# Layer 0's memory keys and values in one pass, x loaded early into the residual's tile, zeros multiplied ahead, and wide products ahead of narrow ones in every weight-stationary group

## The chip, the cores and the metric

The kernel runs on one core of one Trainium2 chip. The metric is the device time of one execution in microseconds (us), as the median of several executions. A difference of under about 0.2% cannot be told from no change by such a measurement.

## The reference, cut to what matters

Two layers. Each projects x (256 rows of 2048) by an input matrix, runs three groups of heads and maps their concatenation back. The change touches the memory group's keys and values, which depend on `mem` (256 tokens of 2048) alone, and how all projections are multiplied:

```python
def hybrid_layer(x, mem, w_in, rel_table, gate_w, gate_b, gla_norm_g, w_mem_kv, w_out, ln_g, ln_b):
    h = x @ w_in
    a_q, a_k, a_v, a_z, b_q, b_k, b_v, b_z, b_lr, m_q, m_z = jnp.split(h, cuts, axis=-1)
    y_a = chunk_band_attention(heads_a(a_q), heads_a(a_k), heads_a(a_v), rel_table).reshape(B, S, A_WIDTH)
    ...                                   # gated linear attention gives y_b
    mkv = mem @ w_mem_kv                  # (256 x 2048) @ (2048 x 1024)
    mk, mv = jnp.split(mkv, 2, axis=-1)   # keys 512 wide, values 512 wide
    y_m = memory_attention(heads_m(m_q), heads_m(mk), heads_m(mv)).reshape(B, S, M_WIDTH)
    y = jnp.concatenate([y_a * jax.nn.silu(a_z), y_b * jax.nn.silu(b_z), y_m * jax.nn.silu(m_z)], axis=-1)
    return layer_norm(DEEPNORM_ALPHA * x + y @ w_out, ln_g, ln_b)
```

## The kernel before

Every operand is split into a high part (`hi`, rounded by ACT's cast, L117) and a low part (`lo`, the rest, by DVE's subtraction, L118); `parts` does both. A product is then hi\*hi + lo\*hi + hi\*lo. The contraction over 2048 is cut into 16 k-tiles of 128.

Two forms of product stand in the kernel. In `as_group` (activation stationary; L194 ff.) a 128x128 block of x or mem is the loaded weight and 512 (or 388) weight columns stream past: three wide matmuls per k-tile and half of the rows, all into one bank. In `ws_half` (weight stationary; L166 ff.) a 128x128 block of the weights is loaded and the tokens stream past: one *wide* matmul of 512 columns (`both`: hi and lo beside each other) and one *narrow* of 256 (`wl` against `xh`), which adds to the second half of the same bank. `ws_group` runs two such halves of 256 output columns; for each of 16 k-tiles a half does two blocks b. There are 11 such groups in a layer: G_MK, G_BQK, four for the attention heads, G_MQ and four gates.

The order on PE and on SP (which issues the DMAs) is the program's own; on ACT and DVE a scheduler sets it. Weights come by `piece` (512 KB each) through a ring of four buffers under the tag `raw` and four each for `wh` and `wl`; an operand x or mem quarter comes by `load_quarter` through the same `raw` ring. SP waits before it reuses a `raw` buffer, until DVE has split what was in it, and before it reuses one of eight DMA semaphores, until the earlier transfer has landed.

Layer 0 starts with G_MV (`as_group` with `begin`; `begin_pieces` loads the first two quarters of mem and the first four pieces of weights in small transfers), then G_MK (`ws_group` on the loaded mem), then G_BQK, whose first half loads x's quarters. `res`, the residual's tile (256x2048 in fp32), is filled from `xn` only after the first two groups of attention values.

Of the kernel before, what the change touches and what calls it, by code (L numbers as in the profile page):

```python
# [18 lines left out]
P = 128  # L19
# [18 lines left out]
def hybrid_trunk_kernel(  # L38
# [50 lines left out]
    def nm(s):  # L89
        uid[0] += 1  # L90
        return f"{s}_{uid[0]}"

    def mm(o, l, r, start, stop):
        pe.matmul(o, l, r, start=start, stop=stop, skip_group_check=True)  # L94
# [15 lines left out]
    def operand():  # L110

        x = opp.tile([P, 4, 2, T], F32R, name=nm("x"), tag="x")
        return x[:, :, 0], x[:, :, 1], x.rearrange("p j h t -> p j (h t)")

    def parts(hi, lo, src):

        act.copy(hi, src)  # L117
        dve.tensor_tensor(lo, src, hi.bitcast(F32), op=ALU.subtract)  # L118
# [24 lines left out]

    def begin_pieces(q, xsrc, wsrc):

        xraw = wp.tile([P, 4, T], F32, name=nm("raw"), tag="raw")
        x = operand()
        xh, xl, _ = x
        w = []
        for pc in range(2):  # L150
            wraw = wp.tile([P, 2, 512], F32, name=nm("raw"), tag="raw")
            wh = wp.tile([P, 2, 512], F32R, name=nm("wh"), tag="wh")
            wl = wp.tile([P, 2, 512], F32R, name=nm("wl"), tag="wl")
            w.append((wh, wl))
            for k in range(2):
                if q == 0 or k == 0:
                    j = slice(pc * 2 + k, pc * 2 + k + (1 if q == 0 else 2))
                    sp.dma_start(xraw[:, j], xsrc[:, j])
                    parts(xh[:, j], xl[:, j], xraw[:, j])
                cut = 2 if q == pc == k == 0 else 1  # L160
                for h in range(cut):
                    cs = slice(h * 512 // cut, (h + 1) * 512 // cut)
                    sp.dma_start(wraw[:, k, cs], wsrc[pc].rearrange("p (k n) -> p k n", k=2)[:, k, cs])
                    parts(wh[:, k, cs], wl[:, k, cs], wraw[:, k, cs])
        return x, w

    def ws_half(src, xq, first=None):

        acc = psd.tile([P, 2, 2, T], F32, name=nm("acc"), tag="acc")
        for pc in range(4):  # L170
            if first is not None:
                xq.append(load_quarter(first[pc]))
# [10 lines left out]
    def ws_group(src, xq, first=None):  # L183

        for half in range(2):
            acc = ws_half(src[half * 4:half * 4 + 4], xq, None if half else first)
            yield half * 2, acc[:, :, 0], acc[:, :, 1]

    def total(dst, a, b, scale=1.0):
        act.mul(dst, b, scale)  # L190
        dve.scalar_tensor_tensor(dst, a, scale, dst, op0=ALU.mult, op1=ALU.add)  # L191

    def as_products(o, t, xq, w, kt, kk):
        wh, wl = w  # L194
        xh, xl, _ = xq[kt // 4]
        j, ts = kt % 4, slice(t * P, (t + 1) * P)
        mm(o, xh[:, j, ts], wh[:, kk], kt == 0, False)
        mm(o, xl[:, j, ts], wh[:, kk], False, False)
        mm(o, xh[:, j, ts], wl[:, kk], False, kt == 15)

    def as_group(src, xq, n, kp=2, first=None, begin=False):

        acc = psd.tile([P, 2, 512], F32, name=nm("acc"), tag="acc")
        for pc in range(16 // kp):
            if begin and pc in (0, 2):
                x, ws = begin_pieces(pc // 2, first[pc // 2], src[pc:pc + 2])
                xq.append(x)
            if begin and pc < 4:
                w = ws[pc % 2]
            else:  # L210
                if first is not None and pc % 2 == 0:
                    xq.append(load_quarter(first[pc // 2]))
                w = piece(src[pc], n, kp)
# [322 lines left out]
    def norm_last(accs, stats, gb, rows):  # L536
# [54 lines left out]
        with tc.manual_schedule(engines={DVE}):  # L591
# [7 lines left out]
            with tc.high_priority(AHEAD):  # L599
# [10 lines left out]
    dve.memset(eps[:, 0:1], LN_EPS)  # L610
    dve.memset(eps[:, 1:2], RMS_EPS)

    attn = [per.tile([P, 4, P], F32, name=f"attn{par}") for par in range(2)]
    for l in range(L):
        mk = [per.tile([P, 4, T], F32R, name=nm("mk"), tag=f"mk{i}") for i in range(2)]
        mv = [per.tile([P, 2, 512], F32R, name=nm("mv"), tag=f"mv{i}") for i in range(2)]
        memq, xq = [], []
        parts(*mv, as_group(w512[l, G_MV], memq, 512, 2, memT, l == 0))
        if l:
            gens = [transposed(xq)]  # L620
            waiting.extend(gens)
        for i, a, b in ws_group(w512[l, G_MK], memq):
            tmp = scratch([P, 2, T])
            total(tmp, a, b)
            parts(mk[0][:, i:i + 2], mk[1][:, i:i + 2], tmp)
        if l:
# [5 lines left out]
        for i, a, b in ws_group(w512[l, G_BQK], xq, None if l else xT):  # L632
            total(gk if i else gq, a, b, 1.0 if i else 0.125)
        gp = gla_inputs(l)
        if l == 0:
# [185 lines left out]
```

## Time and profile before

| | us |
|---|---|
| median of 3 runs | 945.02 (944.0 to 945.37) |
| the profiled execution's time | 944.11 |
| its span, first to last instruction | 942.3 |
| PE busy in it | 927.4 |
| DVE / ACT busy | 584.6 / 497.4 |

The profile's lines name an engine (PE for matmuls, PEld for weight loads, DVE, ACT, POOL, SP), a source line, an operation, and out<-in by tile names without numbers. All matmuls go through one helper and so stand at L94; their tiles tell them apart: `acc<-wh,x` and `acc<-wl,x` are the wide products of `as_group`, `acc<-x,wh` the wide and `acc<-x,wl` the narrow ones of `ws_half`, `bk` a bank of the attention work. A row's duration of a matmul holds its pipeline's drain; the time that one takes from the next is the distance between starts.

### The profile page before, as it was taken

Reading aid. Unit: us, or ns where it says so; the run is one execution under the profiler, and the core shown is the slowest. Engines: PE = TensorE matmul, PEld = TensorE weight load, DVE = VectorE, ACT = ScalarE, POOL = GpSimd, SP = SyncE. Lnnn points to the kernel's source line nnn. Section 1 sums busy time; section 2 is a strip of 40 time slices with the busy share of each in tenths; the row PEclk is TensorE's granted clock in tenths of the full one; section 3 lists DMA queues with packets and bytes.
Section 4 is the critical chain, followed back from the end, with each engine's and each line's share of the span. In section 5 each row is a group of like instructions: output and inputs, shape, how many; then the busy total and the mean of one; then the engine's idle time right before and its main releaser. Section 6 shows DMA issues by size and latency. Waiting matters only on the chain.

```text
span 942.3 us, 14178 instructions
## 1 busy us (share of the span) xinstructions
PE 927.4 (98%) x5506; PEld 812.6 (86%) x5506; DVE 584.6 (62%) x776; ACT 497.4 (53%) x711; POOL 30.4 (3%) x46
## 2 busy tenths in 40 slices
PE   7999999999999999999999999999999999999996
PEld 5889998898888888888878999889888888888884
DVE  5664487555555666555598545965545567566656
ACT  6554475366456665443465346644744576563340
POOL 1000000000000000000031000000000000010000
PEclk9999999999999999999999999999999999999997
DMA  8776865455555466866656465655555445676642
GB/s 267 252 273 177 298 196 167 148 186 167 191 160 162 158 188 194 255 190 193 222 187 227 142 207 177 201 161 176 156 192 173 158 156 159 200 244 205 200 134 89
DMA packets 61459, 178.75 MB, mean 190 GB/s; under 512 B 6824, under 2 KB 18376, under 8 KB 61136
## 3 DMA queue, kind: packets, MB, share of 16 engines
q1 hardware_dynamic: 59664, 173.56, 57.4%
q0 software_dynamic: 1728, 4.28, 1.9%
q8 instruction: 43, 0.70, 0.3%
q14 instruction: 24, 0.20, 0.1%
HBM read 175.69 MB, written 2.10 MB: 189 GB/s over the span
## 4 chain that ended last, share of the span: by engine, by line
PE 91%; DVE 3%; DMA 3%; issue 1%; ACT 1%; SPq 0%; DVEq 0%; ACTq 0%
PE acc L94 83%; PE bk L94 6%; DMA raw<-memT 1%; DVE wl L118 1%; DMA raw<-w 1%; PE bk L424 1%; PE bk L459 0%; DVE stats L499 0%; ACT x L117 0%; PE bk L483 0%; DVE res L518 0%; DVE res L586 0%; DVE res L498 0%; DVE res L519 0%; ACT wh L117 0%
## 5 line engine op out<-in xcount | busy, mean ns | idle before, releaser
L118 DVE TENSOR_TENSOR wl<-raw,wh 128x1024 fp32r<-128x1024 f32 (+3 forms) x325 | 378.0, 1166 | 273.7 <-ACT wh L117 268.2
L117 ACT CAST wh<-raw 128x1024 fp32r<-128x1024 f32 (+3 forms) x325 | 323.1, 995 | 348.8 <-PE acc L94 241.5
L94 PE MATMUL acc<-x,wh 128*128 128x512 f32 x1408 | 505.3, 401 | 0.0
L94 PE MATMUL acc<-x,wl 128*128 128x256 f32 x1408 | 394.7, 280 | 0.2 <-DVE wl L118 0.2
L94 PE MATMUL acc<-wh,x 128*128 128x512 f32 (+1 forms) x1120 | 322.7, 369 | 5.0 <-ACT wh L117 5.0
L94 PEld LDWEIGHTS acc<-x,wh 128*128 128x128 f32 x1408 | 264.3, 188 | 60.4 <-issue 0.3
L94 PEld LDWEIGHTS acc<-x,wl 128*128 128x128 f32 x1408 | 266.0, 189 | 0.9 <-DVE wl L118 0.5
L94 PEld LDWEIGHTS acc<-wh,x 128*128 128x128 f32 x1120 | 207.1, 189 | 31.2 <-ACT wh L117 6.4
L94 PE MATMUL acc<-wl,x 128*128 128x512 f32 (+1 forms) x560 | 206.3, 368 | 1.7 <-DVE wl L118 1.7
L94 PEld LDWEIGHTS acc<-wl,x 128*128 128x128 f32 x560 | 105.6, 189 | 14.9 <-DVE wl L118 2.9
L118 DVE TENSOR_TENSOR x<-raw,x 128x1024 fp32r<-128x1024 f32 (+2 forms) x16 | 15.3, 954 | 19.9 <-ACT x L117 19.9
L117 ACT CAST x<-raw 128x1024 fp32r<-128x1024 f32 (+2 forms) x16 | 13.4, 836 | 22.8 <-DMA raw<-memT 16.2
L416 ACT ACTIVATE sc<-sc,mx 128x128 f32<-128x128 f32 (+1 forms) x32 | 14.4, 450 | 17.8 <-DVE mx L414 17.7
L191 DVE SCALAR_TENSOR_TENSOR sc<-acc,sc 128x512 f32<-128x512 f32 x24 | 16.4, 681 | 0.0
L409 DVE SCALAR_TENSOR_TENSOR sc<-bk,bias 128x384 f32<-128x384 f32 x16 | 8.9, 554 | 10.3 <-PE bk L94 10.3
L190 ACT ACTIVATE sc<-acc 128x512 f32<-128x512 f32 x24 | 14.3, 595 | 0.0
L696 DVE TENSOR_TENSOR sc<-sc,yr 128x512 f32<-128x512 f32 x16 | 11.0, 690 | 5.2 <-ACT sc L692 5.2
L498 DVE SCALAR_TENSOR_TENSOR res<-res,acc 128x512 f32<-128x512 f32 x15 | 9.7, 684 | 7.2 <-PE acc L94 7.2
L94 PE MATMUL bk<-qk,qk 128*128 128x128 f32 (+1 forms) x64 | 13.1, 326 | 0.0
L94 PE MATMUL bk<-sc,asv 128*128 128x256 f32 (+1 forms) x64 | 13.0, 325 | 0.0
L692 ACT ACTIVATE sc<-sc 128x512 f32<-128x512 f32 x16 | 10.1, 629 | 4.6 <-DVE sc L191 4.5
L94 PEld LDWEIGHTS bk<-sc,asv 128*128 128x128 f32 x64 | 11.1, 188 | 1.5
(164 smaller groups left out, 497.6 us busy)
## 6 DMA issues: line engine op xcount, KB each, us to landing
raw<-w SPq DMA_DIRECT2D x236, 512.0 KB, 3.7
raw<-w SPq DMA_DIRECT2D x64, 388.0 KB, 3.1
raw<-w SPq DMA_DIRECT2D x39, 256.0 KB, 3.1
raw<-memT SPq DMA_DIRECT2D x6, 512.0 KB, 4.5
bias<-relw SPq DMA_DIRECT2D x16, 192.0 KB, 3.7
raw<-xT SPq DMA_DIRECT2D x4, 512.0 KB, 4.4
res<-xn SPq DMA_DIRECT2D x1, 2048.0 KB, 9.6
sc<-ln_g POOLq DMA_DIRECT2D x8, 256.0 KB, 5.3
```

The costliest lines, as they stand in the source:

```text
L94: pe.matmul(o, l, r, start=start, stop=stop, skip_group_check=True)
L117: act.copy(hi, src)
L118: dve.tensor_tensor(lo, src, hi.bitcast(F32), op=ALU.subtract)
L190: act.mul(dst, b, scale)
L191: dve.scalar_tensor_tensor(dst, a, scale, dst, op0=ALU.mult, op1=ALU.add)
L409: dve.scalar_tensor_tensor(s, pb[:, :384], SCALE, bias[h], op0=ALU.mult, op1=ALU.add)
L416: act.activation(s[:, own[t]], s[:, own[t]], AF.Exp, bias=mx[:, t:t + 1], accum_out=zs[:, t:t + 1])
L424: pe.transpose(pt[:, i * P:(i + 1) * P], s[:, i * P:(i + 1) * P], ident)
L498: dve.scalar_tensor_tensor(r, r, ALPHA, acc, op0=ALU.mult, op1=ALU.add)
L692: act.activation(sz, sz, AF.Silu)
L696: dve.tensor_tensor(sz, sz, yraw[i][:, j:j + 2], op=ALU.mult)
```

## The change

Four edits:

- Seven fp32 matmuls of a 128x128 tile of zeros by itself, into a bank that is not read, stand at the start of PE's program. DVE clears the tile first.
- `first_memory` takes the place of layer 0's G_MV and G_MK groups. It walks 8 pieces p of two k-tiles each and loads for each two k-tiles of mem, of the value weights and of the key weights. For p = 0 and 1 the values' and keys' products alternate by k-tile; from p = 2 on a piece's values come first, then its keys; the keys of p = 6 are put off until the values of p = 7 are done. Keys fill four banks at once (four blocks b): four wide, then four narrow per k-tile.
- `early` is the residual's tile seen as four quarters. mem's quarters are loaded into it, and x's quarter q once mem's quarter q has been split (`resident_quarter`, after p = 2, 4, 6 and 7). The `raw` ring holds only weights there.
- In `ws_half` a k-tile's two wide products come first, then its two narrow ones, in all other weight-stationary groups of both layers.

```diff
+    def resident_quarter(q, src):
+        with tc.high_priority(AHEAD):
+            x = operand()
+            sp.dma_start(early[:, q], src)
+            parts(x[0], x[1], early[:, q])
+        return x
...
+    def first_memory(mk, mv, each):
...
+        def keys_of(p, w, kk):
+            (wh, wl), (xh, _, both), j = w, memq[p // 2], p % 2 * 2 + kk
+            for b in range(4):
+                mm(blocks[b].rearrange("p h t -> p (h t)"), wh[:, kk, b * P:(b + 1) * P], both[:, j], p == kk == 0, False)
+            for b in range(4):
+                mm(blocks[b][:, 1], wl[:, kk, b * P:(b + 1) * P], xh[:, j], False, p * 2 + kk == 15)
...
+            if p == 6:
+                late = k
+            elif p > 1:
+                if p == 7:
+                    parts(*mv, accv)
+                    for kk in range(2):
+                        keys_of(6, late, kk)
+                for kk in range(2):
+                    keys_of(p, k, kk)
+            each(p)
...
     def ws_half(src, xq):
...
             for j in range(4):
                 for b in range(2):
-                    cs = slice(b * P, (b + 1) * P)
-                    mm(acc[:, b].rearrange("p h t -> p (h t)"), wh[:, j, cs], both[:, j], pc == j == 0, False)
-                    mm(acc[:, b, 1], wl[:, j, cs], xh[:, j], False, pc == j == 3)
+                    mm(acc[:, b].rearrange("p h t -> p (h t)"), wh[:, j, b * P:(b + 1) * P], both[:, j], pc == j == 0, False)
+                for b in range(2):
+                    mm(acc[:, b, 1], wl[:, j, b * P:(b + 1) * P], xh[:, j], False, pc == j == 3)
...
+    zeros = hd.tile([P, P], F32, name="zeros", tag="st")
+    dve.memset(zeros, 0.0)
+    idle = bank()
+    for _ in range(7):
+        mm(idle[:, :P], zeros, zeros, True, True)
+
     res = per.tile([P, 2, D], F32, name="res")
+    early = res.rearrange("p t d -> p (t d)").rearrange("p (q j t) -> p q j t", q=4, t=T)
...
+        if l == 0:
+            def each(p):
+                if p in (2, 4, 6, 7):
+                    xq.append(resident_quarter(len(xq), xT[len(xq)]))
+
+            first_memory(mk, mv, each)
```

How the instructions stand, by engine; numbers behind a name tell buffers apart, and `x2` behind a row that it stands twice.

PE before, where layer 0's values end and its keys begin (acc_97 holds the values, acc_291 the first half of the keys):

```order
L94 MATMUL acc_97<-wh_272,x_249 128x512 x2
L94 MATMUL acc_97<-wl_273,x_249 128x512
L94 MATMUL acc_291<-x_99,wh_293 128x512
L94 MATMUL acc_291<-x_99,wl_294 128x256
L94 MATMUL acc_291<-x_99,wh_293 128x512
```

PE after, at the start of the program (acc_107 holds the values, acc_108, bk_109 and bk_110 the four blocks of the keys):

```order
L94 MATMUL bk_90<-zeros 128x128 x7
L94 MATMUL acc_107<-wh_114,x_111 128x512 x2
L94 MATMUL acc_107<-wl_116,x_111 128x512
L94 MATMUL acc_107<-wh_114,x_111 128x512 x2
L94 MATMUL acc_107<-wl_116,x_111 128x512
L94 MATMUL acc_108<-x_111,wh_115 128x512 x2
L94 MATMUL bk_109<-x_111,wh_115 128x512
L94 MATMUL bk_110<-x_111,wh_115 128x512
L94 MATMUL acc_108<-x_111,wl_117 128x256 x2
L94 MATMUL bk_109<-x_111,wl_117 128x256
L94 MATMUL bk_110<-x_111,wl_117 128x256
```

The keys' first k-tile now stands right behind the values' first, and the zeros ahead of both.

PE before, where G_BQK begins:

```order
L94 MATMUL acc_385<-x_249,wl_454 128x256
L94 MATMUL acc_485<-x_487,wh_492 128x512
L94 MATMUL acc_485<-x_487,wl_493 128x256
L94 MATMUL acc_485<-x_487,wh_492 128x512
L94 MATMUL acc_485<-x_487,wl_493 128x256
```

PE after, at the same place:

```order
L94 MATMUL acc_108<-x_415,wl_453 128x256 x2
L94 MATMUL bk_109<-x_415,wl_453 128x256
L94 MATMUL bk_110<-x_415,wl_453 128x256
L94 MATMUL acc_532<-x_274,wh_534 128x512 x2
L94 MATMUL acc_532<-x_274,wl_535 128x256 x2
```

The two wide products of a k-tile now stand next to each other, and so do the two narrow ones.

SP before, at the start (raw_98 takes mem's first quarter, raw_100 and raw_118 the first two pieces of value weights):

```order
L158 DMA raw_98<-memT 128x256
L163 DMA raw_100<-w 128x256 x2
L158 DMA raw_98<-memT 128x256
L163 DMA raw_100<-w 128x512
L158 DMA raw_98<-memT 128x256
L163 DMA raw_118<-w 128x512
L158 DMA raw_98<-memT 128x256
L163 DMA raw_118<-w 128x512
L158 DMA raw_157<-memT 128x512
```

SP after, at the start (res takes mem and then x, raw_112 and raw_172 value weights, raw_113 and raw_173 key weights):

```order
L163 DMA res<-memT 128x256
L176 DMA raw_112<-w 128x256 x2
L179 DMA raw_113<-w 128x256 x2
L163 DMA res<-memT 128x256
L176 DMA raw_112<-w 128x512
L179 DMA raw_113<-w 128x256 x2
L163 DMA res<-memT 128x256
L176 DMA raw_172<-w 128x512
L179 DMA raw_173<-w 128x256 x2
```

Each k-tile of the start now brings two transfers of key weights behind its value weights, and mem's no longer take a buffer of the `raw` ring.

More of the change, by code (lines that the diff above doesn't have):

```diff
@@ L142, in piece @@
         return hi, lo
[L144 to L165, printed above, removed]
@@ L167, in ws_half, with first_pieces, x_part, split @@
-    def ws_half(src, xq, first=None):
+    def resident_quarter(q, src):
[4 more added lines that the diff above has]
+        return x
+    def first_pieces(p, x):
+        xsrc, j0 = memT[p // 2], p % 2 * 2
+        xraw = early[:, p // 2]
+        vsrc = w512[0, G_MV, p].rearrange("p (k n) -> p k n", k=2)
+        ksrc = [w512[0, G_MK, h * 4 + p // 2][:, j0 * 256:j0 * 256 + 512].rearrange("p (k n) -> p k n", k=2) for h in range(2)]
+        raws, his, los = ([wp.tile([P, 2, 512], dt, name=nm(n), tag=n) for _ in range(2)]
+                          for n, dt in (("raw", F32), ("wh", F32R), ("wl", F32R)))
+        def x_part(j):
+            sp.dma_start(xraw[:, j], xsrc[:, j])
+            parts(x[0][:, j], x[1][:, j], xraw[:, j])
+        def split(i, at):
+            parts(his[i][at], los[i][at], raws[i][at])
+        if p < 2:
+            with tc.manual_schedule(engines={DVE, mybir.EngineType.Activation}):
+                for k in range(2):
+                    x_part(slice(j0 + k, j0 + k + 1))
+                    cut = 2 if p == k == 0 else 1
+                    for h in range(cut):
+                        cs = slice(h * 512 // cut, (h + 1) * 512 // cut)
+                        sp.dma_start(raws[0][:, k, cs], vsrc[:, k, cs])
+                        split(0, (slice(None), k, cs))
+                    for h in range(2):
+                        sp.dma_start(raws[1][:, k, h * 256:(h + 1) * 256], ksrc[h][:, k])
+                    split(1, (slice(None), k))
+        else:
+            with tc.high_priority(AHEAD):
+                x_part(slice(j0, j0 + 2))
+                sp.dma_start(raws[0], vsrc)
+                split(0, slice(None))
+                for h in range(2):
+                    sp.dma_start(raws[1][:, :, h * 256:(h + 1) * 256], ksrc[h])
+                split(1, slice(None))
+        return list(zip(his, los))
@@ new lines, in first_memory, with values_of @@
+    def first_memory(mk, mv, each):
+        memq = []
+        accv = psd.tile([P, 2, 512], F32, name=nm("acc"), tag="acc")
+        acck = psd.tile([P, 2, 2, T], F32, name=nm("acc"), tag="acc")
+        blocks = [acck[:, b] for b in range(2)] + [bank().rearrange("p (h t) -> p h t", h=2) for _ in range(2)]
+        def values_of(p, w, kk):
+            for t in range(2):
+                as_products(accv[:, t], t, memq, w, p * 2 + kk, kk)
+        def keys_of(p, w, kk):
[4 more added lines that the diff above has]
+                mm(blocks[b][:, 1], wl[:, kk, b * P:(b + 1) * P], xh[:, j], False, p * 2 + kk == 15)
+        late = None
+        for p in range(8):
+            if p % 2 == 0:
+                memq.append(operand())
+            v, k = first_pieces(p, memq[-1])
+            for kk in range(2):
+                values_of(p, v, kk)
+                if p < 2:
+                    keys_of(p, k, kk)
[6 more added lines that the diff above has]
+                        keys_of(6, late, kk)
+                for kk in range(2):
+                    keys_of(p, k, kk)
+            each(p)
+        for half in range(2):
+            tmp = scratch([P, 2, T])
+            if half == 0:
+                total(tmp, acck[:, :, 0], acck[:, :, 1])
+            else:
+                for b in range(2):
+                    total(tmp[:, b], blocks[2 + b][:, 0], blocks[2 + b][:, 1])
+            parts(mk[0][:, half * 2:half * 2 + 2], mk[1][:, half * 2:half * 2 + 2], tmp)
@@ L169, in ws_half @@
+    def ws_half(src, xq):
         acc = psd.tile([P, 2, 2, T], F32, name=nm("acc"), tag="acc")
         for pc in range(4):
-            if first is not None:
-                xq.append(load_quarter(first[pc]))
             wh, wl = piece(src[pc], 256, 4)
@@ L176, in ws_half, with ws_group @@
                 for b in range(2):
-                    cs = slice(b * P, (b + 1) * P)
-                    mm(acc[:, b].rearrange("p h t -> p (h t)"), wh[:, j, cs], both[:, j], pc == j == 0, False)
-                    mm(acc[:, b, 1], wl[:, j, cs], xh[:, j], False, pc == j == 3)
+                    mm(acc[:, b].rearrange("p h t -> p (h t)"), wh[:, j, b * P:(b + 1) * P], both[:, j], pc == j == 0, False)
+                for b in range(2):
+                    mm(acc[:, b, 1], wl[:, j, b * P:(b + 1) * P], xh[:, j], False, pc == j == 3)
             tick()
         return acc
-    def ws_group(src, xq, first=None):
+    def ws_group(src, xq):
         for half in range(2):
-            acc = ws_half(src[half * 4:half * 4 + 4], xq, None if half else first)
+            acc = ws_half(src[half * 4:half * 4 + 4], xq)
             yield half * 2, acc[:, :, 0], acc[:, :, 1]
@@ L199, in as_products, with as_group @@
         mm(o, xh[:, j, ts], wl[:, kk], False, kt == 15)
-    def as_group(src, xq, n, kp=2, first=None, begin=False):
+    def as_group(src, xq, n, kp=2, first=None):
         acc = psd.tile([P, 2, 512], F32, name=nm("acc"), tag="acc")
         for pc in range(16 // kp):
[L205 to L213, printed above, removed]
+            if first is not None and pc % 2 == 0:
+                xq.append(load_quarter(first[pc // 2]))
+            w = piece(src[pc], n, kp)
             for kk in range(kp):
@@ L631, in hybrid_trunk_kernel @@
         gk = hd.tile([P, 2, T], F32, name=nm("gk"), tag="gk")
-        for i, a, b in ws_group(w512[l, G_BQK], xq, None if l else xT):
+        for i, a, b in ws_group(w512[l, G_BQK], xq):
             total(gk if i else gq, a, b, 1.0 if i else 0.125)
```

16 lines of the change are left out of this document (8 added, 8 removed).

## The prediction

> **What bounds the kernel now.** I read the page first, its busy times, its chain and its groups:
>
> ```profile
> PE 927.4 (98%) x5506; PEld 812.6 (86%) x5506; DVE 584.6 (62%) x776; ACT 497.4 (53%) x711; POOL 30.4 (3%) x46
> PE 91%; DVE 3%; DMA 3%; issue 1%; ACT 1%; SPq 0%; DVEq 0%; ACTq 0%
> L94 PE MATMUL acc<-x,wh 128*128 128x512 f32 x1408 | 505.3, 401 | 0.0
> L94 PE MATMUL acc<-x,wl 128*128 128x256 f32 x1408 | 394.7, 280 | 0.2 <-DVE wl L118 0.2
> ```
>
> PE is the bound: 91% of the chain is its work, and 1408 wide and 1408 narrow products of the weight-stationary groups are most of its instructions. So there are two ways to gain: less time per product, or less loss where PE waits or runs slowly. The same products stay; what can move is the distance from one to the next. The second reading is by stage, in windows cut near the group boundaries (start, slow clock; rest of the values; keys; G_BQK):
>
> ```profile
> 0.00:9.56 9.56, 4.93 (x12) 3.78 (x13) 4.13 (x13) 5.65 (x11) 2.94 (x9) 1.00 0.68 214
> 9.56:20.00 10.44, 9.51 (x41) 6.95 (x39) 6.85 (x9) 5.69 (x9) 0.00 (x0) 1.00 0.92 303
> 20.00:30.56 10.56, 10.56 (x47) 8.74 (x47) 6.59 (x6) 6.49 (x7) 0.00 (x0) 1.00 0.90 305
> 30.56:52.97 22.41, 22.41 (x128) 19.47 (x127) 15.77 (x15) 13.42 (x15) 0.00 (x0) 1.00 0.77 257
> 52.97:75.65 22.68, 22.68 (x131) 19.65 (x129) 13.82 (x16) 10.85 (x13) 0.00 (x0) 1.00 0.70 235
> ```
>
> In each row the bracketed numbers count instructions (PE, PEld, DVE, ACT, POOL); the last two columns are the DMA engines' share and GB/s. Through the values the DMA engines are 90 to 92% taken at 303 to 305 GB/s; in the keys and G_BQK they have room. The third reading is PE's timeline at the start (start, duration, what, and in brackets a wait):
>
> ```profile
> 4.63 1.22 PE L94 MATMUL acc<-wh,x 128*128 128x512 f32 x2 [4.63 <-ACT wh L117]
> 6.08 1.05 PE L94 MATMUL acc<-wh,x 128*128 128x512 f32 x2
> 6.93 0.63 PE L94 MATMUL acc<-wl,x 128*128 128x512 f32 x1
> 9.49 0.43 PE L94 MATMUL acc<-wl,x 128*128 128x512 f32 x1
> 9.76 0.63 PE L94 MATMUL acc<-wh,x 128*128 128x512 f32 x2
> 18.74 0.73 PE L94 MATMUL acc<-wh,x 128*128 128x512 f32 x2 [0.40 <-ACT wh L117]
> 20.00 0.50 PE L94 MATMUL acc<-wl,x 128*128 128x512 f32 x1 [0.52 <-DVE wl L118]
> ...
> 876.00 0.39 PE L94 MATMUL acc<-wl,x 128*128 128x512 f32 x1
> 902.52 0.39 PE L94 MATMUL acc<-wl,x 128*128 128x512 f32 x1
> ```
>
> Between the last two rows lie 39 groups of three wide products: 26.52/117 = 0.227 us from start to start. At the start the two from 6.08 to 6.93 take 0.425 each. So PE runs at about half speed from its first product at 4.63 until about 9.5, some 4.9 us after it became busy. The values are 96 wide products (16 k-tiles, two halves, three each). The first 12 take 9.76 - 4.63 = 5.13 us, where 12 x 0.227 = 2.72 would do: **2.40 us are lost to the slow clock**. The other 84 take 30.56 - 9.76 = 20.80 (the keys begin at 30.56) against 19.07: **1.73 us lost**, nearly all before 20.00, where two rows show PE waiting for weights.
>
> The fourth reading is the weight-stationary order, wide, narrow, wide, narrow:
>
> ```profile
> 30.33 0.39 PE L94 MATMUL acc<-wl,x 128*128 128x512 f32 x1
> 30.56 0.39 PE L94 MATMUL acc<-x,wh 128*128 128x512 f32 x1
> 30.78 0.28 PE L94 MATMUL acc<-x,wl 128*128 128x256 f32 x1
> 30.90 0.40 PE L94 MATMUL acc<-x,wh 128*128 128x512 f32 x1
> 31.13 0.28 PE L94 MATMUL acc<-x,wl 128*128 128x256 f32 x1
> ...
> 52.81 0.40 PE L94 MATMUL acc<-x,wh 128*128 128x512 f32 x1
> 75.42 0.40 PE L94 MATMUL acc<-x,wh 128*128 128x512 f32 x1
> ...
> 219.72 0.40 PE L94 MATMUL acc<-x,wh 128*128 128x512 f32 x1
> 221.11 0.40 PE L94 MATMUL acc<-x,wh 128*128 128x512 f32 x1
> ...
> 301.58 0.88 PE L94 MATMUL bk<-mk,mq 128*128 128x256 f32 x6
> 302.30 0.40 PE L94 MATMUL acc<-x,wh 128*128 128x512 f32 x1
> ```
>
> From 52.81 to 75.42 stand 64 pairs of wide and narrow, 0.353 us each; from 219.72 to 221.11 four, 0.348 each. I take 0.351 for the kernel. Six narrow ones in a row (301.58 to 302.30) take 0.120 each, about what a narrow one takes alone (30.78 to 30.90, 0.12; 0.117 is left if the wide one before it has 0.234). So narrow behind narrow costs nothing extra, but a wide one behind a narrow one takes about 0.234, not the 0.227 of wide behind wide. The one wide product here that stands behind a wide one (30.56, behind 30.33) takes 0.22, its neighbour at 30.90 takes 0.23: the same direction, though rows of 0.01 us show it poorly.
>
> **The change part by part.**
>
> *Wide, then narrow.* Two pairs cost 2 x 0.351 = 0.702 now. In the new order one wide product stands behind a narrow one (0.234), one behind a wide one (0.227), one narrow behind wide (0.117) and one narrow behind narrow (0.118 to 0.120): 0.696 to 0.698. I take 0.006 saved. There are 21 such groups besides the first layer's keys, 2 halves, 16 k-tiles: 672 x 0.006 = 4.0 us. The keys have four blocks in one row, so three of four wide ones stand behind a wide one: 16 x 3 x 0.0065 = 0.3. Sum 4.3, all on PE and so on the path. Ends: if both wide products took 0.227, 0.014 x 688 = 9.6 saved; if the wide ones stayed at 0.234 whatever stands ahead and the second narrow one took 0.120, 0.003 x 672 = 2 lost. The value is nearest to the rows of wide behind wide.
>
> [...]
>
> *The zeros.* An fp32 product of 128 columns shows as two rows; eight such rows of a transpose by an identity, the mean of such a row, and DVE's first work:
>
> ```profile
> 211.17 1.04 PE L395 MATMUL bk<-ident,sc 128*128 128x128 f32 x8
> ...
> L395 PE MATMUL bk<-ident,sc 128*128 128x128 f32 x16 | 2.1, 272 | 0.0
> ...
> 0.81 0.06 DVE L610 MEMSET eps<- 128x1 f32 x1 [0.81 <-PEq L811]
> ```
>
> One row with its drain is 0.27; the other seven add (1.04 - 0.27)/7 = 0.11 each, so one product is 0.22 at full clock and at most 0.22 x 0.425/0.227 = 0.41 at half. Seven take 1.5 to 2.9 us. DVE clears the tile from 0.81; no row has a clearing of 128 columns, it lies between 0.06 (one column) and DVE's 0.43 for 256 columns below. So PE works on zeros from about 1.1 to at latest 4.2, before data come at 4.63, and delays nothing. If the clock opens 4.9 us after PE became busy, as it did before, it opens near 6.0. PE then loses (6.0 - 4.63) x (1 - 0.227/0.425) = 0.64 us, not 2.40: **1.7 saved**. Ends: 0 (zeros or the gap behind them don't count), 2.4 (open by 4.63).
>
> *One pass over mem.* The chain to the first product doesn't change: mem's first k-tile, two halves of value weights, their casts:
>
> ```profile
> 3.05 0.40 ACT L117 CAST x<-raw 128x256 fp32r<-128x256 f32 x1 [1.03 <-DMA raw<-memT]
> 4.17 0.40 ACT L117 CAST wh<-raw 128x256 fp32r<-128x256 f32 x1 [0.28 <-DMA raw<-w]
> 4.61 0.43 DVE L118 TENSOR_TENSOR wl<-raw,wh 128x256 fp32r<-128x256 f32 x1 [0.26 <-ACT wh L117]
> 16.31 1.05 ACT L117 CAST x<-raw 128x1024 fp32r<-128x1024 f32 x1 [0.65 <-DMA raw<-memT]
> 2.60 0.44 SPq L163 DMA_DIRECT2D raw<-w  x1
> 3.08 0.43 SPq L158 DMA_DIRECT2D raw<-memT  x1
> ```
>
> A k-tile of values needs 0.13 MB of mem and 0.26 MB of weights for 6 x 0.227 = 1.36 us of PE: 289 GB/s, about what the engines gave, hence the waits. With its keys a k-tile needs 0.655 MB for 1.36 + 1.39 = 2.75 us: 238 GB/s. x's 2.1 MB come on top within 44 us, 286 GB/s in all, so the margin is thin. SP issues a transfer each 0.48 us (2.60 to 3.08); the new k-tiles of p < 2 have four, 1.9 us of 2.75, so SP keeps up. The tightest point by bytes is p = 3's values: mem 1.05, values 2.10, keys 1.57, x 0.52, together 5.24 MB. By 9.56 there were 214 x 9.56 = 2.05 MB; at 304 GB/s the rest is in by 20.1, and a cast of 1.05 and the way to it make 21.5. PE is there at 4.63 + 0.64 + 6 x 2.75 = 21.8. At p = 7, 11.53 MB are in by 40.7, ready by 42.1, needed at 43.8. So up to 0.5 us may be waited for at p = 3 and nothing in the queue falls far behind. Of 1.73 I take **1.0 saved**; ends 1.7 and -1.0.
>
> *x into the residual's tile* costs nothing by itself: four transfers, casts and subtractions as before, earlier; `res` is filled from xn only near 100 us. What G_BQK gains is room on the DMA engines that it didn't lack (70% there). At the end of the pass, the values' bank is split behind x's last quarter, under the keys of p = 6 and 7 (5.5 us of PE); the keys' two more totals on ACT and DVE run under G_BQK's first half (11 us). If that cover went, G_BQK's second half would wait for at most those few operations of 0.4 to 0.7 us.
>
> **The sum.** 4.3 + 1.7 + 1.0 = 7.0 us. Against the profiled execution's own time, 944.11 (its span of 942.3 and 1.8 around it), this gives 937.1. The median of the runs is 0.9 above that execution; the sum from there is **938.0**.
>
> **The rivals.**
>
> [...]
>
> *The zeros don't open the clock*: 938.0 + 1.7 = 939.7. No row shows whether a product of zeros counts. [...]
>
> *Slower: the pass starves.* Everything but x's last quarter, 12.06 MB, must be in by about 45.5 (a cast ahead of the last keys, 2.8 us of PE) for PE to end the pass at 49.3: (12.06 - 2.05)/(45.5 - 9.56) = 279 GB/s. Key weights now land in smaller pieces, two transfers for what was one. If the engines gave only 233 GB/s, the pass would end 7 us late and eat all gains; below that the kernel is slower, at 220 GB/s by 2.5 us, near 947.5. The rows with 257 and 235 GB/s don't show such a limit, since the engines had 23 to 30% left.
>
> [...]
>
> **How the numbers follow.** The forecast has 0.60, no early clock 0.18, no gain by order 0.14, both 0.04, starving 0.04. A difference of under 0.2%, 1.9 us, can't be told from none: above 943.1 counts as the same. The forecast and no early clock end below that; of the no-gain-by-order case (942.3, give or take 1) most does. That makes faster 0.87, same 0.09, slower 0.04. The range goes from 934.5 (half of the order's upper end more) to 942.6, which takes in no early clock whole and half of no gain by order; above lie about 0.15, below 0.04.
>
> **What would show it.** The clock: wide products 0.23 apart from about 6 on, not from 9.5. The pass: keys end and G_BQK begins near 50, not near 53.2 (a pair behind 52.81), with no wait of PE over 0.5 us on the way. The order: in G_BQK two starts of wide products 0.227 apart, and a k-tile's four products 0.696 in all; 32 of them then take 22.3 us, not 22.6. I am wrong if the k-tile takes 0.70 still, if wide products are 0.43 apart beyond 8, or if waits for `wh` stand at p = 3 to 7.

## The result, and the profile after

The changed kernel takes **938.58 us** (median of 6 runs, 938.15 to 939.18) against 944.5 us before (6 runs, 943.95 to 945.37). The ratio is 0.9937, with a 95% interval of 0.9924 to 0.995. So the change saves 0.63% or 5.9 us, three times what a measurement here can tell from nothing. Forecast were 938.0, by a saving of 7.0.

The profiled execution took 938.5 us, with a span of 936.4. Its page, the busy times, the chain and the two groups of the weight-stationary products (source line, engine, operation, tiles, count, busy time, mean ns of one, idle time before it):

```profile
PE 926.8 (99%) x5520; PEld 813.9 (87%) x5520; DVE 585.6 (63%) x780; ACT 497.8 (53%) x714; POOL 30.1 (3%) x46
PE 94%; DVE 2%; DMA 2%; issue 1%; ACT 0%; SPq 0%; DVEq 0%
L94 PE MATMUL acc<-x,wh 128*128 128x512 f32 x1376 | 439.4, 401 | 0.0
L94 PE MATMUL acc<-x,wl 128*128 128x256 f32 x1376 | 271.4, 279 | 0.0
```

PE's busy time hardly moves (927.4 before, 926.8 now), though the span is 5.9 shorter. That is no contradiction: PE now works on zeros for over 3 us in which it stood before, and it waits less. The mean of one product also stands (401 ns), because a row runs on past the start of the next (0.39 us long, 0.23 apart) and so does not show the distance; the two groups' busy times fall (505.3 to 439.4, 394.7 to 271.4) because neighbours that belong to one group now overlap and are counted once, and because half of the first layer's keys now stands under `bk`. None of these figures tells the saving; the starts do.

The windows of the start (start of the keys and values, rest of the pass until its end, G_BQK until the first product of the attention values; columns as in the prediction):

```profile
0.00:6.45 6.45, 5.01 (x18) 4.43 (x19) 1.51 (x9) 3.02 (x5) 2.93 (x9) 1.00 0.53 165
6.45:20.00 13.55, 13.52 (x65) 10.93 (x65) 8.88 (x13) 8.52 (x14) 0.00 (x0) 1.00 0.99 328
20.00:50.99 30.99, 30.99 (x159) 26.11 (x158) 24.94 (x23) 20.84 (x24) 0.00 (x0) 1.00 0.91 325
50.99:73.07 22.08, 22.08 (x129) 19.27 (x128) 12.50 (x16) 9.90 (x15) 0.00 (x0) 1.00 0.57 178
```

From 6.45 to 20 us PE is busy but for 0.03 us, and the DMA engines move 325 to 328 GB/s; in the stage windows of before they moved at most 305 (332 in one stretch of 5 us, from 25 on). The pass does not starve. Busy is not full speed, though: a row outlasts the distance to the next start, and by their starts the products between 10 and 30 us are held up by some 0.8 us in sum.

PE's timeline at the start:

```profile
1.05 3.36 PE L94 MATMUL bk<-zeros 128*128 128x128 f32 x14 [1.05 <-DVE nt L606]
4.80 1.22 PE L94 MATMUL acc<-wh,x 128*128 128x512 f32 x2 [0.39 <-ACT wh L117]
6.25 0.73 PE L94 MATMUL acc<-wh,x 128*128 128x512 f32 x2
6.81 0.39 PE L94 MATMUL acc<-wl,x 128*128 128x512 f32 x1
...
50.76 0.63 PE L94 MATMUL acc<-x,wh 128*128 128x512 f32 x2
...
72.37 0.62 PE L94 MATMUL acc<-x,wh 128*128 128x512 f32 x2
73.06 0.34 PE L94 MATMUL acc<-wh,x 128*128 128x388 f32 x1
```

The seven zero products (14 rows) run from 1.05 to about 4.4. From 6.81 on wide products stand 0.23 apart; between 6.25 and 6.81 they take 0.28 each, so the clock opened in there, near 6.45, instead of near 9.5. (The granted clock reads 1.00 in all these windows, before and after, so "the clock", here and below, is a name for what the distances show: 0.427 for a wide product, then 0.227 to 0.236.) G_BQK begins at 50.76, and its first 31 k-tiles take (72.37 - 50.76)/31 = 0.697 us each. The attention values begin at 73.06; before they began at 75.77.

Where the span's 5.9 us lie, from the starts of the same products in both profiles: 2.71 are gained by that point (75.77 to 73.06), a further 1.05 until layer 0's output projection, 1.05 at the boundary of the layers, where a wait of PE shrank, and 1.06 more until the end. The boundary was in no term of the forecast. The executions' own times lie 5.6 apart (944.11 and 938.5).

### The profile page after: what moved, and what is told of

Read it like the earlier page. It is cut to its first block, busy times and chain, and to the rows that moved or that the text cites. A ratio compares the mean times of both kernels' runs of the same rounds, so it can differ in the third digit from the quotient of the medians.

```text
span 936.4 us, 14232 instructions
## 1 busy us (share of the span) xinstructions
PE 926.8 (99%) x5520; PEld 813.9 (87%) x5520; DVE 585.6 (63%) x780; ACT 497.8 (53%) x714; POOL 30.1 (3%) x46
## 4 chain that ended last, share of the span: by engine, by line
PE 94%; DVE 2%; DMA 2%; issue 1%; ACT 0%; SPq 0%; DVEq 0%
PE acc L94 85%; PE bk L94 8%; DMA raw<-memT 1%; PE bk L486 1%; DVE wl L118 0%; PE bk L521 0%; PE bk L545 0%; DVE stats L561 0%; ACT x L117 0%; DVE res L580 0%; DVE res L648 0%; DMA raw<-w 0%; DVE res L560 0%; PE bk L457 0%; DVE x L118 0%
## 5 line engine op out<-in xcount | busy, mean ns | idle before, releaser
L94 PE MATMUL acc<-x,wh 128*128 128x512 f32 x1376 | 439.4, 401 | 0.0
L94 PEld LDWEIGHTS acc<-x,wl 128*128 128x128 f32 x1376 | 258.4, 188 | 61.2 <-DVE wl L118 0.4
L94 PE MATMUL acc<-x,wl 128*128 128x256 f32 x1376 | 271.4, 279 | 0.0
L94 PEld LDWEIGHTS acc<-x,wh 128*128 128x128 f32 x1376 | 211.9, 189 | 2.4 <-issue 0.3
L118 DVE TENSOR_TENSOR x<-res,x 128x512 fp32r<-128x512 f32 (+2 forms) x14 | 10.5, 765 | 5.1 <-ACT x L117 5.1
L117 ACT CAST x<-res 128x512 fp32r<-128x512 f32 (+2 forms) x14 | 9.2, 679 | 4.7 <-DMA res<-xT 3.2
```

## The experiments

**The order alone.** The kernel before, with only `ws_half` changed:

```diff
+                for b in range(2):
+                    mm(acc[:, b]..., wh[:, j, b * P:(b + 1) * P], both[:, j], ...)
                 for b in range(2):
-                    mm(acc[:, b]..., wh[:, j, cs], both[:, j], ...)
-                    mm(acc[:, b, 1], wl[:, j, cs], xh[:, j], ...)
+                    mm(acc[:, b, 1], wl[:, j, b * P:(b + 1) * P], xh[:, j], ...)
```

> The kernel before with one edit: in the weight-stationary halves a k-tile's two wide products come first, then its two narrow ones. The first pass and the start are as before. Theory A (the forecast's): a wide product behind a wide one takes 0.227 us, so 704 k-tiles save 0.006 each, 4.3 us, and the new order's second wide product is 7 ns shorter than its first. Theory B (from the changed kernel's trace): the old order runs in two patterns, 0.693 and 0.707 us per k-tile by place, mean 0.7016, and the new one in one, 0.697, with both wide products at about 0.233; 704 x 0.0043 = 3.0 us saved, little or nothing where the old order ran at 0.693. Theory C: the order is worth nothing, the time stays within 1 us.

Measured: 941.40 against 944.38, ratio 0.9969 (0.9958 to 0.998), so 3.0 us. The same group G_BQK in its timeline, first and last k-tile:

```profile
53.20 0.63 PE L94 MATMUL acc<-x,wh 128*128 128x512 f32 x2
...
74.80 0.63 PE L94 MATMUL acc<-x,wh 128*128 128x512 f32 x2
```

31 k-tiles take 21.60 us, 0.697 each. To see what that replaces, I measured the starts in all undisturbed k-tiles of the kernel before. They come in **two patterns**. One is the pair of the prediction, 0.353 or 0.7066 a k-tile. The other shows in two rows of the kernel before that stand 41 k-tiles apart:

```profile
346.27 0.39 PE L94 MATMUL acc<-x,wh 128*128 128x512 f32 x1
...
374.69 0.39 PE L94 MATMUL acc<-x,wh 128*128 128x512 f32 x1
```

28.42/41 = 0.693: faster than the new order. Of 546 undisturbed k-tiles some 210 are of the fast kind; the mean is 0.7016. The new order has one pattern: nine of ten k-tiles take 0.694 to 0.698. By the mean starts it takes 0.6973; the saving is 0.0043 x 704 k-tiles (the keys' included) = 3.0 us, and the order alone measured 3.0.

Where it sits in a k-tile was a surprise. The two wide products in the new order take 0.233 and 0.233, the narrow ones 0.115 and 0.116. The second wide one, behind a wide one, gains nothing. What goes is the slow pattern, in which the wide ones take 0.233 to 0.241 and the narrow ones 0.113 to 0.120.

**The zeros alone**, on the kernel before:

```diff
+    zeros = hd.tile([P, P], F32, name="zeros", tag="st")
+    dve.memset(zeros, 0.0)
+    idle = bank()
+    for _ in range(7):
+        mm(idle[:, :P], zeros, zeros, True, True)
```

> The kernel before with one edit: seven products of zeros at the start. Theory A: they open the clock some 3 us earlier, products of the first k-tiles are 0.23 apart from 6 to 6.5 us on instead of 9.5; of that 1.4 to 1.7 us reach the end if data keep up. Rival: the old first pass is fed at the rate of the DMA engines (0.90 to 0.92 of them taken), so PE that starts faster only waits for weights sooner: the waits between 9 and 20 us grow from 1.7 us by nearly as much as the clock gives, and the end moves by under 0.5 us.

Measured: 943.83 against 944.38, ratio 0.9998 (0.9989 to 1.0006): nothing. Its PE timeline:

```profile
4.64 0.73 PE L94 MATMUL acc<-wh,x 128*128 128x512 f32 x2 [0.40 <-ACT wh L117]
5.44 0.62 PE L94 MATMUL acc<-wh,x 128*128 128x512 f32 x2
7.20 0.73 PE L94 MATMUL acc<-wh,x 128*128 128x512 f32 x2 [0.92 <-ACT wh L117]
...
16.07 0.73 PE L94 MATMUL acc<-wh,x 128*128 128x512 f32 x2 [0.78 <-ACT wh L117]
...
19.75 0.73 PE L94 MATMUL acc<-wh,x 128*128 128x512 f32 x2 [0.38 <-ACT wh L117]
21.01 0.50 PE L94 MATMUL acc<-wl,x 128*128 128x512 f32 x1 [0.53 <-DVE wl L118]
```

The zeros do what they should: at 5.44 the products already take their full-clock time (two in 0.45, from 5.44 to 5.89), where the kernel before is slow (0.427) until 9.5. The thirteenth of the 14 zero rows is already shorter (0.183 instead of 0.213 to the next start), so here zeros alone opened the clock, 2.9 us after PE's first work. Then the gain is handed back, in waits of 0.92, 0.78, 0.38 and 0.53 for weights. The values alone use 0.39 MB each 1.36 us, and a faster PE reaches sooner the point where the weights are not there. So to this stage, short of data, the early clock gave nothing.

**The pass alone**: the kernel after without the zeros, and with the old alternating order in `ws_half` (the keys inside the pass keep four wide, then four narrow).

```diff
                 for b in range(2):
-                    mm(acc[:, b]..., wh[:, j, b * P:(b + 1) * P], both[:, j], ...)
-                for b in range(2):
-                    mm(acc[:, b, 1], wl[:, j, b * P:(b + 1) * P], xh[:, j], ...)
+                    mm(acc[:, b]..., wh[:, j, cs], both[:, j], ...)
+                    mm(acc[:, b, 1], wl[:, j, cs], xh[:, j], ...)
...
-    for _ in range(7):
-        mm(idle[:, :P], zeros, zeros, True, True)
```

> The changed kernel without the zeros and with wide, narrow, wide, narrow in the other weight-stationary groups: the one pass over mem and the early x alone. Theory A: it takes away the waits for weights before 20 us: 1.0 us saved (0.5 to 1.7). Rival: with the slow clock at the start there was time for data anyway, and the pass saves as much as the zeros don't, so that pass and zeros alone add up to less than the two together (2.7 us to the first group of attention values). The wait of 1.2 us at the layer's boundary (near 479 us before) either goes with this edit or stays.

Measured: 941.54 against 944.38, ratio 0.9967 (0.9956 to 0.9978), so 2.8 us. Rows of its PE timeline:

```profile
5.23 1.22 PE L94 MATMUL acc<-wh,x 128*128 128x512 f32 x2 [5.23 <-ACT wh L117]
...
9.66 0.43 PE L94 MATMUL acc<-x,wl 128*128 128x256 f32 x2
...
479.81 0.50 PE L94 MATMUL acc<-wl,x 128*128 128x512 f32 x1 [1.54 <-DVE wl L118]
```

This execution began late (5.23) and ran on the slow clock until about 9.7; still its G_BQK begins at 51.71, 1.45 us earlier than before (53.16), and no product between 10 and 30 us is held up. In the pass PE needs fewer bytes a microsecond, so what it does slowly it does while data come. The attention values begin at 73.90, 1.9 us earlier than before; the other 0.4 is not the pass, but G_BQK running in the fast one of the two patterns here (0.6935 a k-tile against 0.707). This execution itself took 942.51, the highest of its seven, 1.6 below the profiled one of before; its boundary wait, 1.54 in the row, is as long as before. What else the median's 2.8 holds, this profile does not show.

The three parts alone give 3.0, 0.5 (not told from 0) and 2.8, together 6.3; all at once measured 5.9. They add up within what the intervals leave. Order and pass alone make 5.8 of it.

**The change without its zeros, and the change again**, in one comparison:

```diff
-    for _ in range(7):
-        mm(idle[:, :P], zeros, zeros, True, True)
```

> The changed kernel without the products of zeros; the one pass, the early x and the new order stay. Theory A (the forecast's size): the zeros are worth 1.7 us where data are ahead, so this takes 940.2. Theory B (from the kernels with zeros so far: with the clock open at 4 to 6.5 us, PE waits 0.4 to 1.4 us more for weights before 30 us): the zeros are worth 0.3 to 1.0 us here, 939.0 to 939.6, products are 0.43 apart until 9 to 10.5 us, and the waits for weights between 10 and 30 us fall from 0.9 us to under 0.2.

> The changed kernel itself once more, on this chip and beside the others. Its k-tile in the weight-stationary groups should again be 0.697 in one pattern. Open is the wait at the layer's boundary, 0.29 us in the first profile against 1.33 in the kernel before and 1.0 to 1.7 in three of the single edits. Theory D: it follows the landing of mem's third quarter, which DVE splits ahead of the residual sum, and differs from execution to execution; then this profile may show any value between 0.2 and 1.7, in step with that landing. Theory E: the change as a whole takes it away; then it is 0.2 to 0.4 again.

Measured: without the zeros 939.27 (938.98 to 940.16), ratio 0.994 (0.9924 to 0.9956); with them 938.57 (937.9 to 939.52), ratio 0.9931 (0.9916 to 0.9945). The medians differ by 0.7 us; the intervals overlap. PE's timeline at the start, where G_BQK begins and at the boundary of the layers, first without the zeros, then with them:

```profile
4.70 1.22 PE L94 MATMUL acc<-wh,x 128*128 128x512 f32 x2 [4.70 <-ACT wh L117]
...
8.10 0.63 PE L94 MATMUL bk<-x,wh 128*128 128x512 f32 x2
...
50.57 0.63 PE L94 MATMUL acc<-x,wh 128*128 128x512 f32 x2
...
477.35 0.50 PE L94 MATMUL acc<-wl,x 128*128 128x512 f32 x1 [1.15 <-DVE wl L118]
```

```profile
4.54 1.22 PE L94 MATMUL acc<-wh,x 128*128 128x512 f32 x2
...
6.84 0.52 PE L94 MATMUL acc<-wl,x 128*128 128x512 f32 x1
...
50.26 0.63 PE L94 MATMUL acc<-x,wh 128*128 128x512 f32 x2
...
476.37 0.50 PE L94 MATMUL acc<-wl,x 128*128 128x512 f32 x1 [0.48 <-DVE wl L118]
```

Without zeros the clock opens near 7.9, with them near 7.1 in this execution (6.45 in the other). So most of the zeros' lead of 3.6 us is lost on the way to the clock in these two. From PE's first work to the opening, worked out from the distances of products: 2.9 us (zeros alone), 3.2 (change without zeros), 4.5 (pass alone), 4.9 (before), 5.4 and 6.0 (the change, twice); the other six profiles lie between. With zeros it opened between 3.9 and 7.1 (eight profiles), without them between 7.9 and 10.3 (four). What sets the delay is not shown.

The rows also show that the start does not hold the 0.7 us. Without zeros no product between 10 and 30 us is held up, and G_BQK begins at 50.57. With zeros it begins at 50.76 and 50.26 in the two profiles of the change, and at 50.05 to 50.84 in the four kernels below that share its start (the two longer orders, the other bank, mem's own buffers): what the early clock gives, PE waits for again, even with the pass. Most of what parts these two executions, 0.9 us, is the wait at the boundary, 1.15 against 0.48. So nothing here shows that the early clock saves time; it is worth at most the 0.7 of the medians.

**Four wide, then four narrow**, over two k-tiles, in the kernel after. If a wide product gains by standing behind a wide one, this gains more.

```diff
+            for j0 in (0, 2):
+                for j in (j0, j0 + 1):
+                    for b in range(2):
+                        mm(acc[:, b]..., wh[:, j, b * P:(b + 1) * P], both[:, j], ...)
+                for j in (j0, j0 + 1):
+                    for b in range(2):
+                        mm(acc[:, b, 1], wl[:, j, b * P:(b + 1) * P], xh[:, j], ...)
```

> The changed kernel with the order taken further: in the weight-stationary halves four wide products of two k-tiles, then their four narrow ones. Theory A: three of four wide ones stand behind a wide one, 0.227, so a k-tile takes 0.692 to 0.693, 3 us less than the changed kernel over 672 k-tiles (near 935.5). Theory B (what counts is the pattern that products settle into, not what stands right ahead): 0.693 to 0.70 per k-tile with wide ones still at 0.23, a gain of 0 to 2.5 us. The keys of the one pass, which have four and four, took 1.38 to 1.39 us for eight, 0.690 to 0.695 per four, and would repeat here.

Measured: 939.05 against 944.38, ratio 0.9945 (0.9933 to 0.9958): no better than the change. In G_BQK:

```profile
52.08 1.09 PE L94 MATMUL acc<-x,wh 128*128 128x512 f32 x4
...
53.48 1.09 PE L94 MATMUL acc<-x,wh 128*128 128x512 f32 x4
```

1.40 us for two k-tiles, 0.700 each. The four wide products take 0.234, 0.234, 0.232 and 0.229, the narrow ones 0.117 to 0.119: a wide one comes down only slowly along a row of its kind, and what it gains the narrow ones lose. A kernel with **eight and eight** followed this further (all four k-tiles' wide products, then all narrow ones):

> The changed kernel with eight wide products of a whole piece (four k-tiles), then its eight narrow ones. In the order of four and four, wide products took 0.2335, 0.2335, 0.2315 and 0.2285 in turn, and narrow ones 0.117 to 0.119. Theory I (a wide product comes down to 0.227 only some four products after the last narrow one): here the fifth to eighth wide one take 0.227, a k-tile 0.696, no better than the changed kernel's 0.697. Theory A (forecast): all but the first take 0.227, 0.692.

It took 937.74 in its one execution, within what the change itself shows (937.9 to 939.52). Its G_BQK:

```profile
52.85 2.00 PE L94 MATMUL acc<-x,wh 128*128 128x512 f32 x8
...
69.61 2.00 PE L94 MATMUL acc<-x,wh 128*128 128x512 f32 x8
```

Six groups of four k-tiles in 16.76 us, 0.698 a k-tile. The last three of eight wide products do reach 0.227, and six of the eight narrow ones take 0.120. The three orders tried without single alternation all end at 0.697 to 0.700 in G_BQK. (In later groups of this kernel the first wide product of eight often takes 0.31 to 0.42; why is not shown.)

**Alternating, but each narrow product into the other bank.** The slow pattern could come from a narrow product adding to the bank that the wide one ahead of it has just written. Here each narrow product is held back by one wide:

```diff
                 for b in range(2):
                     mm(acc[:, b]..., wh[:, j, b * P:(b + 1) * P], both[:, j], ...)
-                for b in range(2):
-                    mm(acc[:, b, 1], wl[:, j, b * P:(b + 1) * P], xh[:, j], ...)
+                    if held is not None:
+                        mm(acc[:, 1 - b, 1], *held, ...)
+                    held = wl[:, j, b * P:(b + 1) * P], xh[:, j]
```

> The changed kernel with wide and narrow products alternating again in the weight-stationary halves, but each narrow one is the one held over from the block before, so it adds to the other bank than the wide product right ahead of it. Theory F (adding to the bank just written costs): the slow pattern of the old order, three pairs in 1.06 us, is gone, and a k-tile takes 0.693 to 0.697. Theory G (it is the alternation of wide and narrow itself): both patterns of the old order are there, 0.693 and 0.707, mean near 0.70.

Measured in a single execution: 940.9 us. Both patterns are back, with a mean of 0.702 over all undisturbed k-tiles. In G_BQK:

```profile
51.43 0.39 PE L94 MATMUL acc<-x,wh 128*128 128x512 f32 x1
...
72.77 0.40 PE L94 MATMUL acc<-x,wh 128*128 128x512 f32 x1
```

Between these rows lie 61 pairs, 0.350 each or 0.700 a k-tile: a mix of the two. It is the alternation itself, then, and not the bank. What picks the pattern, 0.693 or 0.707, stays open: the same program text runs in both within one execution.

**The boundary of the layers.** Before layer 1's first products, DVE's queue holds the split of a mem quarter ahead of the sum of the residual; the split waits for ACT's cast, and that for the quarter's transfer. In the kernel before, then after (timelines of ACT, DVE and PE: ACT's cast, DVE's first residual sum, PE's wait):

```profile
468.42 1.05 ACT L117 CAST x<-raw 128x1024 fp32r<-128x1024 f32 x1 [2.93 <-DMA raw<-memT]
470.65 1.28 DVE L498 SCALAR_TENSOR_TENSOR res<-res,acc 128x512 f32<-128x512 f32 x2
481.32 0.50 PE L94 MATMUL acc<-wl,x 128*128 128x512 f32 x1 [1.17 <-DVE wl L118]
```

```profile
463.61 1.05 ACT L117 CAST x<-raw 128x1024 fp32r<-128x1024 f32 x1 [2.80 <-DMA raw<-memT]
465.84 1.28 DVE L560 SCALAR_TENSOR_TENSOR res<-res,acc 128x512 f32<-128x512 f32 x2
476.52 0.50 PE L94 MATMUL acc<-wl,x 128*128 128x512 f32 x1
```

The last product of layer 0's output ended a chain at 465.71 before and 461.95 after, so the cast came 2.71 and 1.66 us behind it, and PE's waits in that place sum to 1.44 and 0.40; in the second profile of the change it is 2.01 and 0.75. The wait follows the landing of that quarter. Over the eleven profiles with this transfer the cast lay between 1.42 and 2.80 behind, and the waits sum to 0.27 to 1.82. They fall into two sets that don't overlap: 0.27 to 0.75 in the six with both the zeros and the pass, 1.09 to 1.82 in the five that lack one or both. To test the chain, layer 1's mem quarters were given buffers of their own, so that they could be loaded far ahead:

```diff
-        raw = wp.tile([P, 4, T], F32, name=nm("raw"), tag="raw")
+        raw = hd.tile([P, 4, T], F32, name=nm("mraw"), tag="qk", bufs=4)
```

> The changed kernel with layer 1's quarters of mem loaded into buffers of their own (those of the heads' q and k, free by then) rather than the weights' ring, so that a quarter's load doesn't wait for a ring buffer. Theory D: the wait at the layer's boundary comes from the landing of mem's third quarter; it falls to 0.2 or less, 0.1 to 1.0 us saved, 937.6 to 938.5. Rival: the residual sum stays behind other splits on DVE, whose order the scheduler sets anew here, and the wait moves but doesn't shrink; the time stays within 0.5 us.

Measured: 940.82 (938.84 to 942.51), ratio 0.9951 (0.9933 to 0.9969): 2.2 us slower than the change. The wait at that place is gone, so the chain is right; but a new one took its place. DVE and PE, then POOL; in the second fence DVE in the change at the same place, and the group of its splits before this stretch:

```profile
477.47 5.87 DVE L581 SCALAR_TENSOR_TENSOR res<-res,rstd,sc 128x512 f32<-128x512 f32 x4
483.26 6.76 DVE L118 TENSOR_TENSOR wl<-raw,wh 128x1024 fp32r<-128x1024 f32 x3
485.62 0.50 PE L94 MATMUL acc<-x,wl 128*128 128x256 f32 x2 [1.43 <-DVE wl L118]
...
484.45 4.50 POOL L578 TENSOR_TENSOR res<-res,sc 128x512 f32<-128x512 f32 x2
```

```profile
479.01 1.23 DVE L118 TENSOR_TENSOR wl<-raw,wh 128x1024 fp32r<-128x1024 f32 x1
480.42 5.49 DVE L581 SCALAR_TENSOR_TENSOR res<-res,rstd,sc 128x512 f32<-128x512 f32 x5
485.83 4.56 DVE L118 TENSOR_TENSOR wl<-raw,wh 128x1024 fp32r<-128x1024 f32 x2
...
L118 DVE TENSOR_TENSOR wl<-raw,wh 128x1024 fp32r<-128x1024 f32 x109 | 133.0, 1223 | 90.6 <-ACT wh L117 90.5
```

With the residual done sooner, the norm's operations (5.87 us for the four in the row) start 3.6 us earlier and come on DVE ahead of a split that the change does before them, the one at 479.01. Here it comes first behind them, at 483.26, and PE waits for it. The three splits behind the norm take 2.3 us each while POOL works, instead of 1.22; but so they do in the change (from 485.83), and in the kernel before, so that alone is not what is new. The profiled execution took 938.89, near the lowest of its six, 0.8 above that of the change beside it: the rows explain no more than this, and the rest of the 2.2 stays open.

**The keys' weights in one transfer.** SP issues one transfer each 0.48 us, and the change gives the start two small ones per k-tile of keys. Here they are one:

```diff
-                    for h in range(2):
-                        sp.dma_start(raws[1][:, k, h * 256:(h + 1) * 256], ksrc[h][:, k])
+                    sp.dma_start(raws[1][:, k].rearrange("p (h n) -> p h n", h=2),
+                                 w512[0, G_MK].rearrange("(h q) p c -> p h q c", h=2)[:, :, p // 2, c0:c0 + 256])
```

> The changed kernel with the two transfers of a k-tile's key weights for p = 0 and 1 joined into one (256 KB, the same 1 KB pieces): 13 transfers instead of 17 for the first four k-tiles. Theory H: SP's issue, one transfer each 0.475 us, paces the data in the first 12 us; the third k-tile's value weights are issued at 4.5 instead of 5.4 us, more is in by 10 us, the waits of 0.2 to 0.6 us between 10 and 20 us shrink to 0.1, and the first group of attention values begins 0.3 to 0.7 us earlier than the 72.6 to 73.1 of the changed kernel. Rival: the engines' rate paces them (0.88 of them taken between 5 and 10 us), and nothing moves by more than 0.2 us.

Measured: 938.38 (937.48 to 938.81), ratio 0.9938 (0.9924 to 0.9951). The windows from 5 to 10 us, the change first, then this kernel; and under each, SP's issue of the third k-tile's value weights:

```profile
5.00:10.00 5.00, 5.00 (x21) 4.16 (x22) 2.92 (x6) 2.58 (x5) 0.00 (x0) 1.00 0.88 254
...
5.44 0.43 SPq L176 DMA_DIRECT2D raw<-w  x1
```

```profile
5.00:10.00 5.00, 4.67 (x22) 3.39 (x22) 2.75 (x5) 2.51 (x6) 0.00 (x0) 1.00 0.95 293
...
4.57 0.43 SPq L176 DMA_DIRECT2D raw<-w  x1
```

SP did limit the data at the start: the weights are issued 0.9 us sooner, and 293 GB/s flow instead of 254 (246 to 264 in the five other profiles with the change's start). The attention values begin at 72.15, 0.4 to 0.9 earlier than in the two profiles of the change. Part of that may be chance: G_BQK begins at 49.84, only 0.2 ahead of the earliest of those six. The median is 0.2 below the change's, which these runs cannot tell from none.

## Why the prediction was right, and where its steps were not

**The order** was forecast at 4.3 and is worth 3.0, and the step behind it fell. It said that a wide product behind a wide one takes 0.227. It takes 0.233 there; among eight in a row only the sixth and later reach 0.227. The 39 groups of three that gave the 0.227 are longer rows of wide products, and the step carried a steady figure to a place where it does not hold. The total came out near, because the base was also read too roughly: 0.702 was right as a mean, but it is a mean of 0.693 and 0.707, and what the new order does is to be rid of the second at the price of the first. The forecast 0.696 for a k-tile met 0.697, and that is luck: the second wide product took 0.006 more than forecast, the narrow ones 0.002 to 0.003 less.

No gain by the order stands in the chances with 0.14 and 942.3 (the other two terms, 2.7, off 945.0), and with 0.04 for no early clock besides. It is excluded: with the order alone the time fell by 3.0 us (ratio 0.9958 to 0.998), and a k-tile went from a mean of 0.7016 to 0.697.

**The zeros** were forecast at 1.7. They gave nothing without the pass, and with it 0.7 by the medians, which the intervals don't tell from none. The step that failed took all that the early clock gives as time saved. That holds only if the data are there, and they weren't, with or without the pass: the zeros alone gave full clock at 5.44 and then four waits, and in the change G_BQK begins about when it does without them (50.76 and 50.26 against 50.57). The other size was one draw of many: the clock was to open 4.9 us after PE became busy, near 6.0, and the delay came out anywhere from 2.9 to 6.0. The rival *the zeros don't open the clock* is excluded by the zeros' own timeline; but its time, 939.7, is nearly what the change without zeros took (939.27), since the open clock saves so little.

**The pass** was forecast at 1.0, from waits of 1.73 before 20 us. Alone it measured 2.8. The step allowed for new waits inside the pass, as they come with an early clock. On the slow clock there were none: the pass needs fewer bytes per microsecond (238 GB/s reckoned for a k-tile, against 289), data catch up while PE is slow (317 GB/s flowed from 5 to 10 us), and all of the old waits go. What the median holds beyond these 1.7 is not shown. Terms 2 and 3 are therefore one sum, 2.7 forecast; by medians they are 5.9 - 3.0 = 2.9, and the pass alone makes 2.8 of it. That this sum came out near is luck in its parts: one term too large, the other too small. The rival that the pass starves is wrong: 328 GB/s flowed where 238 to 286 were needed. The step *SP keeps up* was half right: PE did not run dry, but with fewer transfers the data came sooner. One time in the working is off: p = 7's values were said to be needed at 43.8, which counts p = 6's keys ahead of them though they are put off. Without their 2.8 us it is 41.0, before the 42.1 at which the data were reckoned ready; the 325 GB/s that flowed, where 304 were reckoned, made up for it.

**The boundary** gave 1.05 in the profiled execution and was not foreseen. It differs between executions of one kernel (0.40 and 0.75 for the change), but all six profiles with both zeros and pass (0.27 to 0.75) lie below all five that lack one or both (1.09 to 1.82). That points to the change; by what way it would act on a transfer 460 us later, no run shows, so it stays open. Without it the three terms come to 2.71 + 1.05 + 1.06 = 4.8 in that pair of executions, against the 7.0 forecast. The total of 938.0 against 938.58 thus owes something to luck: terms too large, one too small and a wait that nobody foresaw partly cancelled.

The range's lower end, 934.5, does not follow from the reason given: half of what the order's upper end adds (9.6 - 4.3) is 2.65, which gives 935.3.

*x into the residual's tile* shows no cost, as forecast, though no run has it alone: G_BQK ran without a wait (22.08 busy of 22.08), with the DMA engines at 57% instead of 70%.

## What to carry to other kernels

Read a product's price from the sequence in which it will stand: the same wide product takes 0.227 in a long row, 0.233 beside narrow ones and up to 0.241 in an alternation, and a mean can hide two patterns. A faster PE at the start was worth only what the data behind it allowed: widening the work per byte (the pass) paid 2.8 us by the medians, and the early clock was not seen to pay, before it (0.5 us, not told from 0) or after it (0.7 by the medians, not told from none). A wait that is taken away (mem's buffers) has to be followed to what DVE does next: here operations that came free sooner were put ahead of a split that PE needed.

## What the runs showed of the hardware

- Alternating products of 512 and 256 columns settle in one of two patterns, 0.693 or 0.707 us for two of each, within one execution and without a change of the program or the bank. Two and two, four and four, eight and eight took 0.697 to 0.700 in G_BQK, without the second pattern.
- Products of zeros open the clock: with zeros alone the distance of their rows fell from 0.213 to 0.183 us while PE was still at them, and the wide products behind them stood 0.23 apart from 5.44 on, where those of the kernel before stood 0.427 apart until 9.5. The delay from PE's first work to the opening differed from 2.9 to 6.0 us between executions.
- DVE's split of 128x1024 took 2.3 us while POOL worked on `res` and 1.22 elsewhere; POOL's operation took 2.3 beside the splits and 1.7 just before them, in the kernel before and in the change alike. Why is not shown.
